# A latent RWKV kernel: its chains of two head pairs run half a chain apart, in double steps

## The chip, the cores and the metric

The kernel runs on one core of a Trainium2 chip. The metric is the device time of one launch in microseconds (us). The kernel before took 1387.38 us, the median of three runs (1385.10 to 1389.39). Its profile is of another execution, of 1384.0 us.

The engines are PE (matrix products), DVE (vector), ACT (scalar: functions and copies), POOL and SP (here mostly DMA queues). Each takes its instructions in the order in which they stand in its queue; semaphores tie the queues together.

## What is computed

Two layers of a diffusion backbone over 512 latent tokens of 1024 features, with 256 context tokens ahead. The part that matters is the first layer's time mixing, a recurrence over tokens run forwards and backwards, for 16 heads of 64:

```python
def wkv_scan(S0, r, decay, k, v, kk, a, reverse):
    def step(S, inp):
        r_t, w_t, k_t, v_t, kk_t, a_t = inp
        sa = jnp.einsum("bhvk,bhk->bhv", S, -kk_t)
        S = (S * w_t[:, :, None, :]
             + sa[..., None] * (kk_t * a_t)[:, :, None, :]
             + v_t[..., None] * k_t[:, :, None, :])
        return S, jnp.einsum("bhvk,bhk->bhv", S, r_t)
...
out_f, S_f = wkv_scan(S0_f, rt, tm(decay[0]), tm(kd[0]), vt, kkt, tm(a[0]), False)
out_b, S_b = wkv_scan(S0_b, rt, tm(decay[1]), tm(kd[1]), vt, kkt, tm(a[1]), True)
o = tm(out_f + out_b)
y = head_group_norm(o, lnx_w, lnx_b) + bonus
...
yb = bg * dwconv(cg * xb, sc_w, seg_len)
y = concat([ya * silu(za), yb * silu(zb)]) @ w_out
```

The starting states of the latent scan are the final ones of the same scan over the context. A gated short convolution (`yb`) runs beside it, and one output projection joins both.

## The kernel before

The recurrence is computed in chunks of 64 tokens, two heads (a pair) at a time, both directions z together. A pair goes through these parts, and the names are those of the code and of the profile's tiles:

- `light` (L506 on): per pair and direction, the decays and the scaled factors. Its tiles are sg, al, P and iP (running products of decays and their inverses), kd, bon, AR and BK, partly on ACT, partly on DVE. AR holds two kinds of chunk in turn, A (for the state's own correction) and R (for the output).
- `heavy` (L666 on): the products within chunks, pal, masked into E (DVE, L686); the transposes BKt (ACT, L699); Nt, copied out of E (ACT, L705); UV, into which v goes first.
- `solve` (L729 on): the inverse of a triangular 32 x 32 block, for all chunks at once: a transpose of Nt into Xl (L737), then 62 dependent DVE operations L743 and L745 on X and Y, in turn.
- `merge` (L748 on): two transposes of Y (kdm, am), copies into E, two bursts of 64 small matmuls (mg) with copies between. It makes the 64 x 64 inverses out of the halves.
- `chain_lat` (L836 on): the steps over the eight chunks, one chunk from the front (forwards) and one from the back (backwards) in each. A step takes the states H through six hops: matmuls zol (A H, with products of E and UV begun a step earlier) and onl (R H, the outputs), a copy of zol by ACT (L865), matmuls uh with E's inverses, a copy into UV by ACT (L872), matmuls uh with BKt, and the new H on DVE (L879) from them and HP, the scaled old state that ACT makes (L833). Then the outputs are finished and moved into the tile O, by a copy on ACT (L888) in the first four steps and an add on DVE (L891) in the last four.
- `finish` (L902 on): group norm of O, gate, and the projection's input.

The eight latent pairs are stages s = 4 to 11; a stage's parts are written by the letters in `STAGE[2]`, "OSPLMHFC", after the eight steps of pair s: po(s+1), solve(s+1), prep of s+2, light(s+2), merge(s+1), heavy(s+2), finish(s), and the convolution branch (four projections of 24 matmuls each: cg, xb, bg, zb). A list scheduler in the build orders each engine's instructions by what is ready and by their place in the program; `tc.issue_after` ties the parts of light, heavy and the convolution behind named steps of the running chain (`LIGHT_AFTER`, `HEAVY_AFTER`, `CONV_AFTER`, counted by `st["anchor"]`). `pinned()` (L641 on) keeps a run of matmuls in written order. So in the kernel before one pair's eight single steps and the next pair's solve are in the same stage.

After stage 11 comes the output projection (tiles wr, wh, wl, o) and the second layer, which the change does not touch.

PSUM has eight banks. The chain's use of them is `uh` (one bank, `uhs[0]`, for all pairs) and three rotating ones from `ps_zo` (two of tag zo, and uh1), which also serve merge and finish.

Of the kernel before, what the change touches and what calls it, by code (L numbers as in the profile page):

```python
# [51 lines left out]
def kernel(ctx: ExitStack, tc: tile.TileContext, I: dict, out: bass.AP):  # L52
# [176 lines left out]
    def start():  # L229
# [499 lines left out]
    def solve(st):  # L729
# [44 lines left out]
    def chain_ctx(st, i):  # L774
# [60 lines left out]

    def chain_lat(st, i):  # L836
        nm, p = st["nm"], st["p"]
        UV, E, BKt, AR, PC = st["UV"], st["E"], st["BKt"], st["AR"], st["PC"]
# [26 lines left out]
        S.copy(Zs, zo[:, 0:2, :])  # L865
        ahead = values(i + 1) if i < nch - 1 else []
        for h, z in hz:
            cmm(uh[ZR[1 - h], z, :], E[ZR[1 - h], h, z * nch + cs[z], 0:CH], Zs[ZR[1 - h], z, :])
            if ahead:
                ahead.pop(0)()  # L870
        for h in range(2):
            u_ = S.copy(UV[ZR[1 - h], i : 2 * nch - i : 2 * nch - 1 - 2 * i, ZR[h]], uh[ZR[1 - h], 0:2, :])  # L872
        h_ = None
        if i < nch - 1:
            for h, z in hz[::-1]:
                cmm(uh[ZR[h], 2 + z, :], BKt[z][:, cs[z], ZR[h]], UV[:, z * nch + cs[z], ZR[h]])
            Hn = w("H", f"H{nm}_{i}")[:, 0:P].rearrange("p (z x) -> p z x", z=2)
            for z in range(2):
                h_ = V.scalar_tensor_tensor(out=Hn[:, z, :], in0=uh[:, 2 + z, :],  # L879
                                            scalar=PC[z][:, i : i + 1], in1=HP[:, z, :], op0=ALU.mult, op1=ALU.add)  # L880
# [4 lines left out]
        for h, z in hz:
            cmm(on[ZR[h], oc[z], :], E[:, h, z * nch + cs[z], CH:], UV[:, z * nch + cs[z], ZR[h]], False, z == 1)
        if i < nch // 2:
            S.copy(O[:, i : nch - i : nch - 1 - 2 * i, :], on[:, 2:4, :])  # L888
        else:
            o = O[:, nch - 1 - i : i + 1 : 2 * i + 1 - nch, :]  # L890
            V.tensor_tensor(out=o, in0=on[:, 2:4, :], in1=o, op=ALU.add)  # L891
# [576 lines left out]
```

## Time and profile before

| what | value |
|---|---|
| median of three runs | 1387.38 us |
| profiled execution | 1384.0 us, span 1382.2 us |
| granted PE clock, mean | 0.992 |
| PE busy | 1319.8 us (95%) |
| DVE busy | 986.4 us (71%) |
| ACT busy | 744.4 us (54%) |
| the latent stages | about 484 to 872 us of the span |
| output projection and second layer | from about 872 us |

The span is what the trace covers; the execution's own time is 1.8 us longer. Times in rows of the timeline are us from the span's start; then the duration, the engine, the line, the operation, what it writes and reads, and its shape. In brackets stands the idle time of the engine ahead of it and what ended it. Matmuls are pipelined and their ends are modelled, so starts say more than ends. A window's row gives each engine's busy time, the number of its instructions in brackets, the granted clock, and the DMA engines' share.

### The profile page before, as it was taken

Reading aid. Unit: us, or ns where it says so; the run is one execution under the profiler, and the core shown is the slowest. Engines: PE = TensorE matmul, PEld = TensorE weight load, DVE = VectorE, ACT = ScalarE, POOL = GpSimd, SP = SyncE. Lnnn points to the kernel's source line nnn. Section 1 sums busy time; section 2 is a strip of 40 time slices with the busy share of each in tenths; the row PEclk is TensorE's granted clock in tenths of the full one; section 3 lists DMA queues with packets and bytes.
Section 4 is the critical chain, followed back from the end, with each engine's and each line's share of the span. In section 5 each row is a group of like instructions: output and inputs, shape, how many; then the busy total and the mean of one; then the engine's idle time right before and its main releaser. Section 6 shows DMA issues by size and latency. Waiting matters only on the chain.

```text
span 1382.2 us, 29703 instructions
## 1 busy us (share of the span) xinstructions
PE 1319.8 (95%) x11925; PEld 975.1 (71%) x11925; DVE 986.4 (71%) x2304; ACT 744.4 (54%) x1509; POOL 127.7 (9%) x263
## 2 busy tenths in 40 slices
PE   6999999999998999999999989999999999999998
PEld 2657777777666766666666666677777787788886
DVE  5857879867999499999999998458653653644323
ACT  6546476555765476675756755547742432554222
POOL 4142200001101010101101000010000000000000
PEclk9999999999999999999999999999999999999999
DMA  9865522222323322223222221578621321133232
GB/s 334 272 215 198 161 62 75 92 75 77 96 86 88 97 76 73 78 66 86 77 72 78 76 72 48 187 264 284 203 70 53 122 74 49 62 116 98 92 99 84
DMA packets 139754, 158.54 MB, mean 115 GB/s; under 512 B 15503, under 2 KB 104223, under 8 KB 139497
## 3 DMA queue, kind: packets, MB, share of 16 engines
q1 hardware_dynamic: 123152, 106.47, 24.9%
q0 software_dynamic: 15856, 49.12, 10.9%
q8 instruction: 93, 1.52, 0.5%
q10 hardware_dynamic: 608, 1.06, 0.2%
q14 instruction: 45, 0.37, 0.1%
HBM read 138.33 MB, written 18.28 MB: 113 GB/s over the span
## 4 chain that ended last, share of the span: by engine, by line
PE 46%; DVE 12%; ACT 7%; issue 4%; DMA 4%; POOL 0%; SPq 0%; DVEq 0%; ACTq 0%; POOLq 0%
PE pu L57 12%; PE pz L57 6%; PE f L57 6%; PE pxb L57 3%; PE pcg L57 3%; PE uh L57 3%; PE o L57 2%; DVE E L686 2%; DMA wr<-in_ev_w_out_dram 2%; PE pzb L57 1%; PE zol L57 1%; PE onl L57 1%; PE px L57 1%; PE pc L57 1%; DVE Yl L745 1%
## 5 line engine op out<-in xcount | busy, mean ns | idle before, releaser
L57 PE MATMUL o<-wh,y 128*128 128x512 f32 x248 | 79.8, 396 | 0.0
L743 DVE TENSOR_TENSOR xtmpl<-Xl,Yl 128x126 f32<-128x126 f32 (+22 forms) x248 | 62.3, 251 | 3.1
L745 DVE TENSOR_TENSOR Yl<-Yl,xtmpl 128x126 f32<-128x126 f32 (+22 forms) x248 | 62.2, 251 | 2.9
L1281 ACT CAST ah<-a 64x512 fp32r<-64x512 f32 x32 | 19.8, 618 | 74.8 <-DVE a L1276 74.4
L57 PEld LDWEIGHTS uh<-UV,BKt 128*64 128x64 f32 x704 | 26.4, 136 | 37.6 <-ACT UV L872 27.8
L57 PEld LDWEIGHTS o<-wh,y 128*128 128x128 f32 x248 | 46.2, 188 | 9.5
L57 PE MATMUL pal<-ARl,BKl 64*128 64x128 f32 x512 | 44.5, 295 | 8.7 <-DVE E L686 7.3
L57 PE MATMUL o<-wl,y 128*128 128x512 f32 x124 | 49.7, 401 | 2.3 <-DVE wl L130 2.3
L872 ACT COPY UV<-uh 64x128 f32<-64x128 f32 x128 | 33.3, 260 | 28.9 <-PE uh L57 26.6
L57 PEld LDWEIGHTS pal<-ARl,BKl 64*128 64x128 f32 x512 | 35.3, 191 | 18.8 <-issue 11.1
L130 DVE TENSOR_TENSOR wl<-wr,wh 128x1024 fp32r<-128x1024 f32 x28 | 34.2, 1223 | 19.1 <-ACT wh L129 19.0
L1276 DVE TENSOR_TENSOR a<-pu,a 128x512 f32<-128x512 f32 x16 | 11.0, 691 | 50.0 <-PE pu L57 47.7
L57 PE MATMUL uh<-UV,BKt 128*64 128x64 f32 x704 | 36.5, 232 | 8.7 <-ACT UV L872 4.5
L686 DVE TENSOR_TENSOR E<-pal,maskE 128x512 f32<-128x512 f32 x64 | 42.9, 684 | 0.3
L1233 DVE SCALAR_TENSOR_TENSOR pr<-px,dbe,What 119x512 f32<-119x512 f32 x32 | 22.6, 746 | 26.6 <-PE px L57 26.6
L129 ACT CAST wh<-wr 128x1024 fp32r<-128x1024 f32 x28 | 29.6, 1056 | 19.3 <-DMA wr<-in_ev_w_out_dram 10.1
L57 PEld LDWEIGHTS uh<-Ol,E 64*64 64x64 f32 x512 | 20.3, 133 | 25.8 <-ACT Ol L865 23.6
L879 DVE SCALAR_TENSOR_TENSOR Hl<-uh,PCl,HPl 128x64 f32<-128x64 f32 x112 | 26.2, 276 | 13.7 <-PE uh L57 5.2
L833 ACT ACTIVATE HPl<-Hl,PCl 128x64 f32<-128x64 f32 x96 | 28.1, 340 | 11.0 <-DVE Hl L879 9.8
L745 DVE TENSOR_TENSOR Yc<-Yc,xtmpc 128x126 f32<-128x126 f32 (+22 forms) x124 | 31.5, 254 | 3.1
L743 DVE TENSOR_TENSOR xtmpc<-Xc,Yc 128x126 f32<-128x126 f32 (+22 forms) x124 | 31.5, 254 | 3.0
L57 PEld LDWEIGHTS zol<-Hl,ARl 64*64 64x64 f32 x448 | 18.0, 134 | 21.0 <-DVE xtmpl L743 5.4
(1002 smaller groups left out, 4284.1 us busy)
## 6 DMA issues: line engine op xcount, KB each, us to landing
wr<-in_ev_w_out_dram SPq DMA_DIRECT2D x28, 512.0 KB, 5.2
mwr<-in_mod_w_dram POOLq DMA_DIRECT2D x28, 256.0 KB, 4.2
wrv<-in_ev_w_in_dram SPq DMA_DIRECT2D x16, 256.0 KB, 2.9
ectx<-in_mod_w_dram POOLq DMA_DIRECT2D x16, 256.0 KB, 4.4
wrr<-in_ev_w_in_dram SPq DMA_DIRECT2D x16, 256.0 KB, 2.9
wrza<-in_ev_w_in_dram SPq DMA_DIRECT2D x16, 256.0 KB, 2.8
wrcg<-in_ev_w_in_dram SPq DMA_DIRECT2D x16, 256.0 KB, 2.9
wrxb<-in_ev_w_in_dram SPq DMA_DIRECT2D x16, 256.0 KB, 2.9
```

The costliest lines, as they stand in the source:

```text
L57: env["pe"] = T.matmul(o, lhsT, rhs, start=start, stop=stop)
L129: S.copy(hi, raw)
L130: env["lo"].tensor_tensor(out=lo, in0=raw, in1=hi, op=ALU.subtract)
L686: st["ev"].append(V.tensor_tensor(out=E[:, h, z * NLAT + c0 : z * NLAT + c0 + m, :], in0=pas[h], in1=maskE[:, z * (1 + h) : z * (1 + h) + ...
L743: V.tensor_tensor(out=tv, in0=X[:, :i, i : i + 1].to_broadcast([P, i, m]), in1=Y[:, i : i + 1, c0:].to_broadcast([P, i, m]), op=ALU.mult)
L745: V.tensor_tensor(out=Y[:, :i, c0:], in0=Y[:, :i, c0:], in1=tv, op=ALU.add)
L833: S.activation(t[:, z, :], H[:, z, :], AF.Copy, scale=st["PC"][z][:, i : i + 1])
L872: u_ = S.copy(UV[ZR[1 - h], i : 2 * nch - i : 2 * nch - 1 - 2 * i, ZR[h]], uh[ZR[1 - h], 0:2, :])
L879: h_ = V.scalar_tensor_tensor(out=Hn[:, z, :], in0=uh[:, 2 + z, :], scalar=PC[z][:, i : i + 1], in1=HP[:, z, :], op0=ALU.mult, op1=ALU.add)
L1233: V.scalar_tensor_tensor(out=pr[s][:NPROD], in0=px[s][:NPROD], scalar=dbe[:, 0:1], in1=What[:, n * 512 : n * 512 + 512], op0=ALU.add, op1= ...
L1276: V.tensor_tensor(out=a, in0=pp[1], in1=a, op=ALU.mult)
L1281: S.copy(ahl[s][hr], a[hr])
```

## The change

The chains of two neighbouring pairs now run together, half a chain apart. Stage 4 first runs four single steps of pair 0 alone. Then each stage's letters are "OSMXPLHFC": solve(s+1) and merge(s+1) first, then X, which is four double steps: the steps 4 to 7 of pair s beside the steps 0 to 3 of pair s+1. Stage 11 ends with four single steps of the last pair.

`chain_lat` becomes a generator that yields between its hops, and `together` takes its two generators in turn, so the two pairs' instructions alternate in the program hop by hop. All its matmuls go through one `pinned()` list, `lat2["go"]`, which fixes their order on PE.

Each of the two pairs has, by its parity, two banks of its own: X (zol's sums, one of the `uhs`) and Y (one of the two zo banks, kept for the whole stretch; tiles zy). Y holds the second product uh in columns 0 and 1, the state product in 2 and 3, and the outputs in 4 and 5. H has two tiles and HP one, each split in halves by parity. The outputs of a step are computed and moved out in the next step (`closing`), ahead of that step's uh matmuls. The tile O is gone: AR becomes one tile for both directions (three buffers of twice the size in place of six), and the copies Zs and the outputs are written into the chunks of it that have been used. `merge` of a later pair works in the solve's X and Y tiles in place of kd, a and P, and in the bank that is the pair's X. Small tiles elsewhere that borrowed AR's buffers (tok, dh, wk1, we) are cut out of the wider tile.

```diff
-STAGE = ("KLSMVHvF", "OPLSMHF", "OSPLMHFC")
+STAGE = ("KLSMVHvF", "OPLSMHF", "OSMXPLHFC")
...
-    NBUF = {"tmp": 3, "bon": 3, "AR": 6, "BK": 2, "BKt": 4, "UV": 2, "E": 2, "PC0": 4, "PC1": 4, "rnq": 2,
+    NBUF = {"tmp": 3, "bon": 3, "AR": 3, "BK": 2, "BKt": 4, "UV": 2, "E": 2, "PC0": 4, "PC1": 4, "rnq": 2,
...
+        if st["lat"] and st["p"]:
+            Xt, Yt = st["XY"]
+            R1, R2, Gs = (t.rearrange("p (a b) -> p a b", b=32) for t in (Xt[:, 0:512], Xt[:, 512:], Yt))
...
-        pg = px = ps_zo("mg" + nm)
+        pg = px = uhs[1 - st["p"] % 2] if st["lat"] else uhs[1]
...
+    lat2 = {"go": pinned()}
...
+            st["py"] = lat2["y"][par]
+            st["xy"] = ch3(uhs[1 - par]), ch3(lat2["y"][par])
+            *st["hn"], st["hp"] = [t[:, par * P : par * P + P].rearrange("p (z x) -> p z x", z=2) for t in lat2["h"]]
...
+        def outs(i, H):
+            cs = (i, nch - 1 - i)
+            oc = (4, 5) if i < nch // 2 else (5, 4)
+            first = [(lambda h=h, z=z: go(Y[ZR[h], oc[z], :], AR[z][ZR[h], cs[z], CH:], H[ZR[h], z, :], z == 1, False))
+                     for z in (1, 0) for h in (1, 0)]
+            then = [(lambda h=h, z=z: go(Y[ZR[h], oc[z], :], E[:, h, z * nch + cs[z], CH:],
+                                         UV[:, z * nch + cs[z], ZR[h]], False, z == 1)) for h, z in hz]
+
+            def evict():
+                if i < nch // 2:
+                    S.copy(Q[:, 2 * i + 1 : 32 - 2 * i : 30 - 4 * i, :], Y[:, 4:6, :])
+                else:
+                    o = Q[:, 15 - 2 * i : 18 + 2 * i : 2 + 4 * i, :]
+                    V.tensor_tensor(out=o, in0=Y[:, 4:6, :], in1=o, op=ALU.add)
...
+        yield
+        Zs = Q[:, 2 * i : 31 - 2 * i : 30 - 4 * i, :]
+        S.copy(Zs, X[:, 0:2, :])
+        yield
+        closing([], then, evict)
+        yield
         ahead = values(i + 1) if i < nch - 1 else []
...
+    def together(*steps):
+        run = [chain_lat(st, i) for st, i in steps]
+        while run:
+            run = [g for g in run if next(g, run) is not run]
...
+        elif s == 4:
+            for i in range(NLAT // 2):
+                together((st, i))
         if s == 11:
+            for i in range(NLAT // 2, NLAT):
+                together((st, i))
             finish(st)
             break
...
+            elif x == "X":
+                for i in range(NLAT // 2):
+                    together((st, i + NLAT // 2), (sts[s + 1], i))
```

The order of DVE's queue before, inside the stage in which pair 3's chain runs. Hl is the new state; xtmpl, Xl and Yl belong to the solve of the next pair; rnql, rrl, kkl and Pl are light's.

```order
L745 TENSOR_TENSOR Yl_8155<-Yl_8155,xtmpl_8156 128x17x8
L502 TENSOR_TENSOR rnql_8244<-rnql_8244 128x16
L879 SCALAR_TENSOR_TENSOR Hl_1_7942<-uh_125,PCl_6600,HPl_1_7909 128x64
L879 SCALAR_TENSOR_TENSOR Hl_1_7942<-uh_125,PCl_6629,HPl_1_7909 128x64
L743 TENSOR_TENSOR xtmpl_8156<-Xl_8154,Yl_8155 128x128
L503 TENSOR_TENSOR rnql_8244<-rnql_8244 128x16
L745 TENSOR_TENSOR Yl_8155<-Yl_8155,xtmpl_8156 128x16x8
L504 SCALAR_TENSOR_TENSOR rnql_8244<-rnql_8244 128x16
L743 TENSOR_TENSOR xtmpl_8156<-Xl_8154,Yl_8155 128x135
L562 STREAM_TRANSPOSE rrl_8256<-rnql_8244 128x512
L745 TENSOR_TENSOR Yl_8155<-Yl_8155,xtmpl_8156 128x15x9
L565 SCALAR_TENSOR_TENSOR kkl_8258<-kl_8222,cols_68,rrl_8256 128x512
```

The same engine after, at the end of the solve of pair 3 (line numbers are those of the changed code: Hl is L920, the outputs' add L878, the merge L755 to L774, light's scan L599). zy_5339 is the bank Y of pair 2, in its second half, and zy_5340 that of pair 3.

```order
L745 TENSOR_TENSOR Yl_7075<-Yl_7075,xtmpl_7076 128x16
L755 STREAM_TRANSPOSE Xl_7074<-Yl_7075 128x32x16
L756 STREAM_TRANSPOSE Xl_7074<-Xl_7074 128x512
L760 COPY E_4885<-Xl_7074 32x16x32 x2
L769 COPY Yl_7075<-uh_125 32x512
L774 COPY E_4885<-uh_125 32x16x32
L920 SCALAR_TENSOR_TENSOR Hl_5341<-zy_5339,PCl_5916,HPl_5343 128x64
L920 SCALAR_TENSOR_TENSOR Hl_5341<-zy_5339,PCl_5945,HPl_5343 128x64
L920 SCALAR_TENSOR_TENSOR Hl_5341<-zy_5340,PCl_6717,HPl_5343 128x64
L920 SCALAR_TENSOR_TENSOR Hl_5341<-zy_5340,PCl_6746,HPl_5343 128x64
L599 SCALAR_TENSOR_TENSOR Pl_7542<-scm,sg 128x528
L878 TENSOR_TENSOR ARl_5923<-zy_5339,ARl_5923 128x2x64
```

The state rows have moved from between the solve's rows to behind the merge, in fours, and the rows beside them are light's wide ones.

ACT's queue before, around two steps of a chain (HPl, then the copy Ol of zol, then UV; al, kdl, iPl, Pl, PCl are light's):

```order
L833 ACTIVATE HPl_5_8891<-Hl_4_8888,PCl_7438 128x64
L833 ACTIVATE HPl_5_8891<-Hl_4_8888,PCl_7467 128x64
L865 COPY Ol_8713<-zol_5_8873 128x128
L610 ACTIVATE kdl_9145<-al_9136,oka,hka 128x512
L603 ACTIVATE iPl_9140<-Pl_9138 128x512
L872 COPY UV_4160<-uh_125 64x2x64 x2
L604 ACTIVATE Pl_9138<-Pl_9138 128x528
L606 COPY PCl_9143<-Pl_9138 128x8
L833 ACTIVATE HPl_6_8927<-Hl_5_8924,PCl_7438 128x64
L833 ACTIVATE HPl_6_8927<-Hl_5_8924,PCl_7467 128x64
```

ACT's queue after, the second double step of X with pairs 3 and 4 (L899 is the copy Zs, L875 the outputs' copy, L910 the copy into UV):

```order
L837 ACTIVATE HPl_5343<-Hl_5341,PCl_7518 128x64
L837 ACTIVATE HPl_5343<-Hl_5341,PCl_7547 128x64
L899 COPY ARl_6724<-uh_125 128x2x64
L899 COPY ARl_7525<-uh_126 128x2x64
L595 ACTIVATE al_8341<-lal_8338,hcol 128x512
L875 COPY ARl_7525<-zy_5339 128x2x64
L601 ACTIVATE iPl_8345<-Pl_8343 128x512
L910 COPY UV_4884<-zy_5340 64x2x64 x2
L602 ACTIVATE Pl_8343<-Pl_8343 128x528
L910 COPY UV_4143<-zy_5339 64x2x64 x2
L604 COPY PCl_8348<-Pl_8343 128x8
L608 ACTIVATE kdl_8350<-al_8341,oka,hka 128x512
```

Two pairs' copies now stand in one step, and light's four wide rows stand between them as they stood between one pair's.

More of the change, by code (lines that the diff above doesn't have):

```diff
@@ L249, in start @@
         dft = w("xtmp", "dft")[:31, :NPROD]
-        tokt = [w("AR", f"tok{j}") for j in range(6)]
+        tokt = [t[:, D * j : D * j + D] for t in [w("AR", f"tok{j}") for j in range(3)] for j in range(2)]
         for j in range(6):
@@ L786, in values @@
         def values(i):
-            st["zo"] = zo = ps_zo(f"zo{nm}_{i}")
+            st["zo"] = zo = ps.tile([P, 512], F32, tag="zo", name=f"zo{nm}_{i}", bufs=2)
             return [(lambda k=k, z=z, c=c, h=h: cmm(four(zo)[ZR[1 - h], k, :], E[ZR[h], h, z * NLAT + c, :],
@@ L834, in scale_H @@
         return t
+    lat2 = {"go": pinned()}
     def chain_lat(st, i):
-        nm, p = st["nm"], st["p"]
+        p, nch = st["p"], NLAT
         UV, E, BKt, AR, PC = st["UV"], st["E"], st["BKt"], st["AR"], st["PC"]
-        uh, nch = ch3(uhs[0]), NLAT
         if i == 0:
+            par = p % 2
+            if "y" not in lat2:
+                lat2["y"] = [ps.tile([P, 512], F32, tag="zo", name=f"zy{x}", bufs=2) for x in range(2)]
+                lat2["h"] = [w(t, f"{t}l{x}") for x, t in enumerate(("H", "H", "HP"))]
+            st["py"] = lat2["y"][par]
+            st["xy"] = ch3(uhs[1 - par]), ch3(lat2["y"][par])
+            *st["hn"], st["hp"] = [t[:, par * P : par * P + P].rearrange("p (z x) -> p z x", z=2) for t in lat2["h"]]
@@ L851, in values @@
             cs = (i, nch - 1 - i)
-            return [(lambda h=h, z=z: cmm(zo[ZR[1 - h], z, :], E[ZR[h], h, z * nch + cs[z], 0:CH],
-                                          UV[ZR[h], z * nch + cs[z], ZR[h]], z == 0, False)) for h, z in hz]
+            return [(lambda h=h, z=z: go(X[ZR[1 - h], z, :], E[ZR[h], h, z * nch + cs[z], 0:CH],
+                                         UV[ZR[h], z * nch + cs[z], ZR[h]], z == 0, False)) for h, z in hz]
+        def outs(i, H):
[8 more added lines that the diff above has]
+                    S.copy(Q[:, 2 * i + 1 : 32 - 2 * i : 30 - 4 * i, :], Y[:, 4:6, :])
+                else:
+                    o = Q[:, 15 - 2 * i : 18 + 2 * i : 2 + 4 * i, :]
+                    V.tensor_tensor(out=o, in0=Y[:, 4:6, :], in1=o, op=ALU.add)
+            return first, then, evict
@@ L855, in chain_lat, with closing @@
+        def closing(first, then, evict):
+            for f in first + then:
+                f()
+            evict()
         if i == 0:
-            for go in values(0):
-                go()
-        zo, on = st["zo"], ch3(ps_zo(f"on{nm}_{i}"))
+            for f in values(0):
+                f()
+        first, then, evict = st.get("outs") or ([], [], lambda: None)
         for z in (1, 0):
             for h in range(2):
-                m0_ = cmm(zo[ZR[1 - h], z, :], AR[z][ZR[h], cs[z], 0:CH], H[ZR[h], z, :], False, z == 0)
-                cmm(on[ZR[1 - h], oc[z], :], AR[z][ZR[1 - h], cs[z], CH:], H[ZR[1 - h], z, :], z == 1, False)
+                m0_ = go(X[ZR[1 - h], z, :], AR[z][ZR[h], cs[z], 0:CH], H[ZR[h], z, :], False, z == 0)
+                if first:
+                    first.pop(0)()
@@ L869, in chain_lat @@
             if ahead:
                 ahead.pop(0)()
+        yield
         for h in range(2):
-            u_ = S.copy(UV[ZR[1 - h], i : 2 * nch - i : 2 * nch - 1 - 2 * i, ZR[h]], uh[ZR[1 - h], 0:2, :])
+            u_ = S.copy(UV[ZR[1 - h], i : 2 * nch - i : 2 * nch - 1 - 2 * i, ZR[h]], Y[ZR[1 - h], 0:2, :])
         h_ = None
+        yield
+        st["outs"] = outs(i, H)
         if i < nch - 1:
             for h, z in hz[::-1]:
-                cmm(uh[ZR[h], 2 + z, :], BKt[z][:, cs[z], ZR[h]], UV[:, z * nch + cs[z], ZR[h]])
@@ L877, in chain_lat @@
-            Hn = w("H", f"H{nm}_{i}")[:, 0:P].rearrange("p (z x) -> p z x", z=2)
+                go(Y[ZR[h], 2 + z, :], BKt[z][:, cs[z], ZR[h]], UV[:, z * nch + cs[z], ZR[h]])
+            yield
+            Hn = st["hn"][i % 2]
             for z in range(2):
-                h_ = V.scalar_tensor_tensor(out=Hn[:, z, :], in0=uh[:, 2 + z, :],
+                h_ = V.scalar_tensor_tensor(out=Hn[:, z, :], in0=Y[:, 2 + z, :],
                                             scalar=PC[z][:, i : i + 1], in1=HP[:, z, :], op0=ALU.mult, op1=ALU.add)
@@ L883, in chain_lat @@
                 st["HP"] = scale_H(st, Hn, i + 1)
+        else:
+            closing(*st["outs"])
         st.setdefault("anc", []).append([x.ins for x in (m0_, u_, h_) if x is not None])
[L885 to L891, printed above, removed]
+    def together(*steps):
+        run = [chain_lat(st, i) for st, i in steps]
+        while run:
+            run = [g for g in run if next(g, run) is not run]
     def gate(p, cb, nm):
@@ L1123, in early @@
         else:
-            hl = [w(tag, f"we{k}{x}", F32R) for x in "hl"]
+            t = w(tag, f"we{k}", F32R)
+            hl = [t[:, x * D : x * D + D] for x in range(2)]
         return y, yr, [w("BK", f"wre{k}")[:, 0:D]] + hl
```

52 lines of the change are left out of this document (23 added, 29 removed).

## The prediction, before the result was known

> **What bounds the kernel now.** The page first, for the engines' totals and for what lies around the span.
>
> ```profile
> span 1382.2 us, 29703 instructions
> PE 1319.8 (95%) x11925; PEld 975.1 (71%) x11925; DVE 986.4 (71%) x2304; ACT 744.4 (54%) x1509; POOL 127.7 (9%) x263
> ```
>
> PE looks like the bound, but that is a mean over unlike stages. The change touches the eight latent head pairs, so next come the transposes of `solve` (one opens each pair's solve; tile Xl), which give the period of a stage, and then the busy time in windows cut at them.
>
> ```profile
> L737 DVE STREAM_TRANSPOSE Xl<-Nt x6: 1975/2025/2084, 528.4 to 820.2; 128x1024 f32<-128x1024 f32 x6
> core 0: us, PE busy (x) PEld busy (x) DVE busy (x) ACT busy (x) POOL busy (x), PEclk, DMA share, GB/s
> 484.50:528.40 43.90, 42.18 (x496) 28.76 (x496) 41.90 (x142) 29.25 (x74) 4.04 (x8) 1.00 0.23 68
> 528.40:820.20 291.80, 275.00 (x4019) 191.59 (x4020) 275.35 (x790) 188.42 (x447) 30.90 (x56) 1.00 0.26 75
> 820.20:872.00 51.80, 49.64 (x716) 33.81 (x716) 39.67 (x117) 25.82 (x67) 2.60 (x5) 0.97 0.20 61
> 872.00:911.00 39.00, 38.62 (x484) 25.97 (x480) 23.33 (x54) 23.10 (x61) 1.09 (x2) 1.00 0.63 204
> ```
>
> Six transposes make five periods of 291.80 / 5 = 58.4 us. DVE is busy for 275.35 / 5 = 55.1 of each and idle for 3.3. Its queue is what the stage costs: PE's 94% is mostly small matmuls whose modelled ends overlap. After 820 DVE falls to 77% and then 60%, and PE takes over (38.62 of 39.00).
>
> Third, what DVE is busy with: the solve's chain of dependent pairs, alone and with something between.
>
> ```profile
> 660.27 0.29 DVE L745 TENSOR_TENSOR Yl<-Yl,xtmpl 128x126 f32<-128x126 f32 x1
> 660.48 0.17 DVE L503 TENSOR_TENSOR rnql<-rnql 128x16 f32<-128x16 f32 x1
> 660.59 0.30 DVE L743 TENSOR_TENSOR xtmpl<-Xl,Yl 128x136 f32<-128x136 f32 x1
> 710.35 0.26 DVE L743 TENSOR_TENSOR xtmpl<-Xl,Yl 128x100 f32<-128x100 f32 x1
> 710.65 0.26 DVE L745 TENSOR_TENSOR Yl<-Yl,xtmpl 128x100 f32<-128x100 f32 x1
> ```
>
> An independent neighbour starts 0.08 before the end of the operation ahead of it (660.27 + 0.29 against 660.48); a dependent one 0.04 after it (710.61 against 710.65). Fourth, one step of a latent chain, which in the kernel before runs between such rows.
>
> ```profile
> 658.75 0.27 PE L57 MATMUL zol<-Hl,ARl 64*64 64x64 f32 x1
> 659.26 0.27 ACT L865 COPY Ol<-zol 128x128 f32<-128x128 f32 x1 [0.23 <-PE zol L57]
> 659.80 0.27 PE L57 MATMUL uh<-Ol,E 64*64 64x64 f32 x1
> 660.31 0.53 ACT L872 COPY UV<-uh 64x128 f32<-64x128 f32 x2 [0.78 <-PE uh L57]
> 660.89 0.45 PE L57 MATMUL uh<-UV,BKt 128*64 128x64 f32 x8
> 661.48 0.48 DVE L879 SCALAR_TENSOR_TENSOR Hl<-uh,PCl,HPl 128x64 f32<-128x64 f32 x2 [0.16 <-ACT sg L590]
> 662.04 0.59 ACT L833 ACTIVATE HPl<-Hl,PCl 128x64 f32<-128x64 f32 x2
> 662.17 0.27 PE L57 MATMUL zol<-Hl,ARl 64*64 64x64 f32 x1
> ```
>
> Six hops: 0.51 + 0.54 + 0.51 + 0.58 + 0.59 + 0.69 = 3.42 us, of which DVE works 0.48. Eight steps are far under 58.4, and the solve's rows stand in the gaps. So the chain's latency is hidden now; what a change must not do is leave DVE idle.
>
> **The change part by part.** *The count of DVE work* hardly moves: the order has 155 rows between two transposes before and after. So I take 55.1 us as a steady stage's work and ask where DVE idles. The rows shown with the change say it: before, the state rows (Hl) stand singly among solve rows; after, all solve rows come first, then the five merge rows with nothing between, then four double steps with only light's rows, then E rows and the transpose. The first half of the next pair's chain needs that merge, so X cannot start before it, and the next solve's rows stand behind X in DVE's queue. What the chain hid behind is gone.
>
> *A double step.* Two loops share ACT's queue and DVE's. The pair of H rows takes 0.48 and the next row starts 0.08 before its end; so with A's H at 0, B's is at 0.40, the four HP rows (0.59 a pair) run to 1.28 (as after 661.48), two Zs copies to 1.82, UV of A from 2.33 and of B to 3.39, B's BKt at 3.44 and its H at 4.03: 3.6 us bare, instead of 6.84 for two single steps. Light's rows stand in the same queues:
>
> ```profile
> 661.33 0.67 ACT L597 ACTIVATE al<-lal,hcol 128x512 f32<-128x512 f32 x1
> L610 ACT ACTIVATE kdl<-al,oka,hka 128x512 f32<-128x512 f32 x8 | 6.5, 813 | 0.0
> L604 ACT ACTIVATE Pl<-Pl 128x528 f32<-128x528 f32 x8 | 5.1, 644 | 0.1
> L637 ACT COPY BKl<-BKl 64x512 f32<-64x512 f32 x8 | 4.9, 617 | 0.1
> L601 DVE TENSOR_TENSOR_SCAN Pl<-scm,sg 128x528 f32<-128x528 f32 x8 | 10.0, 1254 | 0.3 <-ACT sg L593 0.2
> L891 DVE TENSOR_TENSOR Ol<-onl,Ol 128x128 f32<-128x128 f32 x16 | 4.5, 282 | 3.3 <-PE onl L57 3.3
> L686 DVE TENSOR_TENSOR E<-pal,maskE 128x512 f32<-128x512 f32 x32 | 21.2, 685 | 0.2
> ```
>
> First step: sg (as al, 0.67) between the two UV copies, less slack, 4.0. Second: al, the outs' copy (0.27) and iP (as P, 0.64) ahead of A's UV, P ahead of B's: +1.7, 5.3. Third: kd's 0.81 delays HP, and three wide DVE rows stand ahead of the out add, for which, as both use one bank, A's next uh matmul waits (it did not have to, with `on` in a bank of its own): +1.2, 4.8. Fourth: BK's 0.62 between the Zs copies, 4.3. X is 18.4. DVE's work in it: seven pairs of H at 0.40, 2.8; scan 1.2; four out adds 1.1; nine wide rows, as E 0.685 less the 0.08 that neighbours share, 5.4: together 10.5. **Idle in X: 7.9.**
>
> *The merge.* Its rows as they stand before, with others between:
>
> ```profile
> 687.36 1.11 DVE L751 STREAM_TRANSPOSE kdml<-Yl 128x512 f32<-128x512 f32 x1
> 688.98 0.71 DVE L752 STREAM_TRANSPOSE aml<-kdml 128x512 f32<-128x512 f32 x1
> 689.72 0.85 DVE L756 COPY E<-kdml 32x512 f32<-32x512 f32 x2
> 689.83 1.20 PE L57 MATMUL mgl<-aml,E 32*32 32x32 f32 x64 [0.30 <-DVE aml L752]
> 691.98 0.70 DVE L765 COPY Pml<-mgl 32x512 f32<-32x512 f32 x1
> ```
>
> With nothing between them, DVE waits for each of the two mgl bursts: 1.20 less the 0.85 of copies, and 1.20 again, with 0.1 at four hand-overs: **1.9 idle**.
>
> *The transpose's wait.* Nt is copied after the last E; on DVE, weights' and finish's rows stood between.
>
> ```profile
> 701.16 2.50 ACT L705 COPY Nt<-E 32x512 f32<-32x512 f32 x4 [1.55 <-DVE E L686]
> 703.69 1.98 DVE L737 STREAM_TRANSPOSE Xl<-Nt 128x1024 f32<-128x1024 f32 x1 [0.49 <-ACT Nt L705]
> ```
>
> The last two or three of the four copies follow the last E: some 2 us of the 2.50, in which one row of 0.6 stays as cover: **1.4 idle**. *Lost neighbours:* in the order of a stage a solve row follows the other directly 33 times, where it did 11 to 21 times, so some 17 lose the row between. With it the pair went at 0.32 (660.27 to 660.59); alone at 0.30, and the 0.17 row costs 0.17 less 0.08 elsewhere: 0.07 more, 0.09 for the larger tile: **1.5**. [...]
>
> Sum: 7.9 + 1.9 + 1.4 + 1.5 = 12.7 of idle where 3.3 was, a stage of 55.1 + 12.7 = 67.8, **+9.4, five times: +47**.
>
> *The first stage* (484.50 to 528.40): DVE's 41.90 gets what now comes ahead of the next transpose, eight H (1.7) and the merge (4.1 by the rows above, its last copy as Pml): 47.7 + 12.7 = 60.4, **+16.5**.
>
> *The tail* from 820.2: X runs there once without light, and four of the last pair's steps leave the output projection, where PE is full. About 1 us of PE a step (0.27 + 0.27 + 0.45 and overlaps) against X's waits of some 2 us: **-2**, bounds -6 and +4.
>
> Edits at nothing: one AR tile for both directions (same bytes), merge on Xt and Yt (dead after the solve), fixed order of the chain's matmuls (PE waits for ACT there anyway; if not, a matmul of 0.40 is late).
>
> Sum: 47 + 16.5 - 2 = +62 on the profiled execution's 1384.0 (1382.2 of span and 1.8 around it, taken as unchanged), that is 1446. It lies 3.4 under the median 1387.38, so **1449** as a median.
>
> **The rivals.** *Milder:* every double step bare (4 x 3.6, idle 3.9), the merge covered, no lost neighbours: 55.1 + 3.9 + 1.4 = 60.4, five times +2.0, the first stage 47.7 + 5.3 = 53, +9, tail -6: 1387.4 + 13 = 1400. It needs light's ACT rows to fall between the hops.
>
> *Faster:* the double step removes DVE's waits instead of adding some. If a double step is no longer than DVE's work in it (10.5 / 4 = 2.6 us), X idles nothing; with merge and transpose covered, a stage is 55.1 and gives -3.3 six times and -4 in the tail, 1387.4 - 24 = 1363; half of that is 1375. It decides at 2.6 us for two steps; one alone has 3.42 of hops. For it speaks that ACT, whose rows lengthen three of the four steps, is free for a third of the stage (188.42 of 291.80 busy).
>
> *The clock.* This chain-only stretch of before has one, with the H rows on either side:
>
> ```profile
> 827.00:830.40 3.40, 2.09 (x36) 1.49 (x36) 3.13 (x10) 2.53 (x7) 0.08 (x1) 0.98 0.07 22
> 830.40:833.90 3.50, 3.50 (x38) 1.93 (x36) 2.74 (x10) 0.87 (x4) 1.00 (x2) 0.53 0.51 152
> 828.32 0.27 PE L57 MATMUL uh<-Ol,E 64*64 64x64 f32 x1 [1.31 <-ACT Ol L865]
> 829.99 0.48 DVE L879 SCALAR_TENSOR_TENSOR Hl<-uh,PCl,HPl 128x64 f32<-128x64 f32 x2
> 835.31 0.47 DVE L879 SCALAR_TENSOR_TENSOR Hl<-uh,PCl,HPl 128x64 f32<-128x64 f32 x2 [1.97 <-PE uh L57]
> ```
>
> After 3.4 us at 61% PE the granted clock was 0.53, and the step took 5.3 us, 1.9 over the 3.42 of the step above. X has PE about half busy for 18 us. Halved throughout it would cost 1.9 x 4 steps x 6 stages = 46; as the low stretch here ends after 3.5 us, I price three steps in four: +34, 1483. For it, that row; against it, double steps bring twice the matmuls. The Trainium skill (TensorE: Matmul & The Clock Gate, "Why this matters for your kernels") asks only for no idle gap over some 3 us; by that the clock stays whole, yet here it halved with 1.31 us as the idle time before that matmul.
>
> *Not half a chain apart:* A's wait for the out add, or ACT's order, makes the pairs run one after the other: 6.84 a step, X 27.4, idle 16.9 + 4.8, a stage 76.8: five times +18.4, the first +25.5, tail -2, 1503.
>
> **How the numbers follow.** Forecast 0.65, milder 0.11, clock 0.10, one after the other 0.03, faster 0.07, no change by offsets I don't see 0.04. The range runs from the milder case, 1400, to the clock's, 1483; the rest outside is 0.14 and some of each edge. A measurement of this kernel tells 0.3% (4 us) from no change. Faster 0.07, within 0.04, slower 0.89.
>
> **What would show it.** Transposes 67.8 us apart (64 to 71); DVE idle in X near 8 us, released by PE's zy matmuls and ACT's UV; a double step of 4 to 5.3, H to H; the first transpose after the first chain near 545; clock whole in X. A period under 60 makes the prediction wrong: then rows from beside X fill it, or double steps are under 3 us.

## The result, and the profile after

The changed kernel takes 1541.25 us, the median of four runs (1531.00 to 1545.66), against 1387.68 for the kernel before (four runs). The ratio is 1.1108, with a 95% interval of 1.1051 to 1.1165: 154 us slower, where +62 was forecast and 1483 was the upper end. The profiled execution took 1531.0 us. Its page, in the first lines and the row of the granted clock in 40 slices:

```profile
span 1529.2 us, 29756 instructions
PE 1368.5 (89%) x11925; PEld 1039.4 (68%) x11925; DVE 1004.6 (66%) x2304; ACT 749.2 (49%) x1509; POOL 128.0 (8%) x263
PEclk9999999989999787776868795969999999999999
```

The clock row is the news. Before, it was 9 throughout; now it falls to between 5 and 8 in most slices of the latent stages (from the 14th to the 27th). The transposes that open the solves, and the window between the first and the last of them:

```profile
L737 DVE STREAM_TRANSPOSE Xl<-Nt x6: 2046/2056/2059, 566.1 to 964.0; 128x1024 f32<-128x1024 f32 x6
566.10:964.00 397.90, 305.62 (x3860) 230.95 (x3859) 283.83 (x780) 190.63 (x444) 30.21 (x54) 0.77 0.18 53
```

Five periods are 397.9 us, 79.6 each, in place of 58.4. Five times 21.2 is 106 of the 147 us by which the span grew. The stage ahead of them (from the first H at 491.45 to 566.1) grew from 43.9 to 74.7, +31; what lies before the first H, which the change hardly touches, +7 in this execution (e3 below, with the same program up to there, has its first H at 483.8, where it was before); the tail +3.

DVE's work in a period is 283.83 / 5 = 56.8 (55.1 before); its idle time is 22.8 where 12.7 was forecast. One stage, cut at its phases: the solve's last part (657 to 679), the merge, the wait for the first H, the double steps, and the rest:

```profile
657.00:667.00 10.00, 10.00 (x45) 7.87 (x44) 10.00 (x35) 6.83 (x12) 0.49 (x1) 1.00 0.37 108
667.00:674.00 7.00, 2.38 (x11) 1.65 (x9) 6.82 (x19) 2.05 (x4) 0.00 (x0) 0.86 0.24 68
674.00:679.30 5.30, 0.00 (x0) 0.00 (x0) 4.68 (x20) 0.00 (x0) 0.00 (x0) 0.50 0.20 58
679.30:687.70 8.40, 3.84 (x128) 3.57 (x128) 3.95 (x6) 2.38 (x4) 0.54 (x1) 0.50 0.01 2
687.70:692.00 4.30, 3.56 (x64) 2.89 (x64) 0.01 (x1) 1.84 (x6) 0.00 (x0) 0.50 0.22 61
692.00:698.20 6.20, 5.65 (x100) 4.61 (x100) 3.05 (x8) 5.61 (x19) 0.54 (x1) 0.50 0.04 13
698.20:706.70 8.50, 8.29 (x113) 6.31 (x113) 4.88 (x13) 3.60 (x12) 1.60 (x3) 0.50 0.26 73
706.70:714.70 8.00, 7.80 (x110) 5.55 (x111) 2.61 (x8) 3.65 (x12) 2.38 (x4) 0.60 0.18 57
714.70:727.00 12.30, 11.82 (x122) 8.77 (x121) 11.07 (x28) 4.99 (x10) 0.57 (x1) 1.00 0.14 44
```

Read the columns of PE and the clock together. From 669.4 to 681.1 PE has nothing to do, and the clock goes to half at 672 (read in windows of 1 us). It stays there through the merge and X until 713, although PE is 91 to 98% busy in the last 20 us of that. X (687.7 to 714.7) takes 27.0 us, DVE works 10.55 of them. In PE's timeline, the two bursts of the merge with PE's last row ahead of them:

```profile
669.00 0.39 PE L57 MATMUL pxb<-hlh,wlxb 128*128 128x512 f32 x1
681.12 1.92 PE L57 MATMUL uh<-Xl,E 32*32 32x32 f32 x64 [11.74 <-DVE Xl L756]
684.45 1.92 PE L57 MATMUL uh<-Xl,Yl 32*32 32x32 f32 x64 [1.41 <-DVE Yl L769]
```

The convolution's projection xb has ended 12 us before the merge's first burst. A burst that took 1.20 takes 1.92. The merge and the double steps on DVE:

```profile
679.26 1.06 DVE L755 STREAM_TRANSPOSE Xl<-Yl 128x512 f32<-128x512 f32 x1
687.02 0.69 DVE L774 COPY E<-uh 32x512 f32<-32x512 f32 x1 [2.63 <-ACT E L774]
692.02 0.48 DVE L920 SCALAR_TENSOR_TENSOR Hl<-zy,PCl,HPl 128x64 f32<-128x64 f32 x2 [4.31 <-PE zy L57]
698.17 0.47 DVE L920 SCALAR_TENSOR_TENSOR Hl<-zy,PCl,HPl 128x64 f32<-128x64 f32 x2
706.69 0.48 DVE L920 SCALAR_TENSOR_TENSOR Hl<-zy,PCl,HPl 128x64 f32<-128x64 f32 x2 [2.25 <-PE zy L57]
708.04 0.48 DVE L920 SCALAR_TENSOR_TENSOR Hl<-zy,PCl,HPl 128x64 f32<-128x64 f32 x2 [0.88 <-PE zy L57]
714.72 0.47 DVE L920 SCALAR_TENSOR_TENSOR Hl<-zy,PCl,HPl 128x64 f32<-128x64 f32 x2
```

The merge takes 8.45 us (forecast 6.0 by its terms). The steps of the older pair, from H to H, take 6.2 and 8.5, those of the newer one (693.3, 699.6, 708.04, 714.72) 6.3, 8.5 and 6.7, and DVE waits for PE.

### The profile page after: what moved, and what is told of

Its sections match the earlier page's. It is cut to its first block, busy times and chain, and to the rows that moved or that the text cites. A ratio compares the mean times of both kernels' runs of the same rounds, so it can differ in the third digit from the quotient of the medians.

```text
span 1529.2 us, 29756 instructions
## 1 busy us (share of the span) xinstructions
PE 1368.5 (89%) x11925; PEld 1039.4 (68%) x11925; DVE 1004.6 (66%) x2304; ACT 749.2 (49%) x1509; POOL 128.0 (8%) x263
## 4 chain that ended last, share of the span: by engine, by line
PE 49%; DVE 14%; ACT 6%; issue 4%; DMA 4%; POOL 0%; SPq 0%; DVEq 0%; ACTq 0%; POOLq 0%
PE pu L57 12%; PE zy L57 6%; PE pz L57 6%; PE f L57 6%; PE uh L57 4%; PE pcg L57 3%; DVE xtmpl L743 2%; PE pxb L57 2%; DVE Yl L745 2%; PE o L57 2%; PE pzb L57 2%; PE pal L57 2%; DMA wr<-in_ev_w_out_dram 1%; DVE E L686 1%; ACT UV L910 1%
## 5 line engine op out<-in xcount | busy, mean ns | idle before, releaser
L57 PE MATMUL uh<-Xl,E 32*32 32x32 f32 x448 | 13.4, 237 | 72.9 <-DVE Xl L756 72.9
L920 DVE SCALAR_TENSOR_TENSOR Hl<-zy,PCl,HPl 128x64 f32<-128x64 f32 x112 | 26.5, 278 | 63.7 <-PE zy L57 55.5
L57 PEld LDWEIGHTS uh<-Xl,E 32*32 32x32 f32 x448 | 12.5, 151 | 75.8 <-DVE Xl L756 75.8
L57 PE MATMUL pal<-ARl,BKl 64*128 64x128 f32 x512 | 53.2, 328 | 5.3 <-DVE E L686 5.0
L910 ACT COPY UV<-zy 64x128 f32<-64x128 f32 x128 | 33.3, 260 | 27.4 <-PE zy L57 25.7
L57 PE MATMUL uh<-UV,E 64*64 64x64 f32 x512 | 34.7, 294 | 9.8 <-DVE E L774 9.8
L57 PE MATMUL zy<-UV,BKt 128*64 128x64 f32 x448 | 33.9, 296 | 7.4 <-ACT UV L910 7.3
L705 ACT COPY Nt<-E 32x512 f32<-32x512 f32 x32 | 19.8, 617 | 40.8 <-DVE E L686 40.5
L57 PEld LDWEIGHTS zy<-UV,BKt 128*64 128x64 f32 x448 | 25.0, 190 | 19.9 <-ACT UV L910 14.9
L57 PEld LDWEIGHTS zy<-ARl,E 64*64 64x64 f32 x512 | 26.0, 186 | 15.7 <-ACT ARl L875 7.1
```

The lines of the kernel that those rows point to most:

```text
L57: env["pe"] = T.matmul(o, lhsT, rhs, start=start, stop=stop)
L705: S.copy(Nt[rs], E[rs, h, :, 32 * b : 32 * b + 32])
L920: h_ = V.scalar_tensor_tensor(out=Hn[:, z, :], in0=Y[:, 2 + z, :], scalar=PC[z][:, i : i + 1], in1=HP[:, z, :], op0=ALU.mult, op1=ALU.add)
```

## The experiments

Two theories stood at the start. *Clock:* the halved clock makes X PE-bound; whole, the stage would be near the forecast 67.8. *Order:* X and the merge stand bare in the queues, and the clock is a side effect.

**The clock, with work that isn't needed.** e3 adds 39 matmuls of 128x512 per stage, three behind each of the last 13 adds of the solve, into a bank that nobody reads; nothing is left out.

```diff
+    def warm(st):
+        t = ps_mm(f"dum{st['nm']}")
+        for x in st["sv"][FROM:]:
+            with tc.issue_after(x.ins):
+                for k in range(PER):
+                    e = mm(t, hlat[0][:, 0, 0:P], hlat[0][:, 1, :], True, True)
+                    if k == 0:
+                        tc.add_manual_dep(e.ins, x.ins.name, ...)
```

> The changed kernel with 39 further matmuls of 128x512 per stage (into a bank nobody reads), three behind each of the last 13 of the solve's 31 adds, so that PE has work until the merge. Clock theory: the 11.7 us in which PE had nothing halve the clock, and X at half clock is bound by PE; kept whole, the merge takes 6 to 7 us in place of 8.4 and X 18 to 21 in place of 27.2, the period falls from 79.6 to 69 to 73 and the time to 1470 to 1495. Rival, order alone: clock or not, the hops and ACT's queue set X; the time stays within 1% of 1541. Third: X's small matmuls can't hold the clock by themselves; then it falls within X again and the period is 74 to 78.

Measured: 1479.55, ratio 1.0676 (1.0637 to 1.0714), clock 0.984. Its transposes, the windows of the filling, the merge and X, and a stretch within X:

```profile
L738 DVE STREAM_TRANSPOSE Xl<-Nt x6: 2041/2050/2055, 552.9 to 914.6; 128x1024 f32<-128x1024 f32 x6
650.00:657.00 7.00, 7.00 (x23) 5.15 (x22) 6.28 (x23) 0.41 (x1) 0.00 (x0) 0.70 0.14 40
657.00:666.00 9.00, 9.00 (x158) 6.95 (x157) 3.22 (x6) 3.01 (x5) 0.54 (x1) 1.00 0.06 10
666.00:677.00 11.00, 10.28 (x237) 7.67 (x236) 6.37 (x16) 9.07 (x30) 0.53 (x1) 1.00 0.15 49
677.00:686.00 9.00, 7.71 (x159) 5.66 (x156) 7.45 (x17) 5.86 (x20) 3.98 (x7) 1.00 0.51 149
671.30:677.40 6.10, 5.78 (x144) 4.55 (x144) 4.85 (x11) 5.67 (x20) 0.66 (x2) 1.00 0.04 13
```

The period is 361.7 / 5 = 72.3, within the expectation, and the clock is whole from the merge to X's end. With it the loss falls from 154 to 94 us: some 60 hang on the clock. But xb's matmuls had moved too, from the solve into the merge and the first part of X, so this run alone can't say which of the large matmuls held the clock. In the last row none of 128x512 starts, and the clock stays whole: there X's small matmuls hold it by themselves.

**The filling alone.** e5 puts 24 such matmuls into the bank of the next merge, so that xb stays ahead.

> As e3, but 24 filling matmuls, two behind each of the last 12 adds of the solve, into the bank that the next merge will use, so that xb stays where it was (in e3 its matmuls had moved into the merge and X). With a whole clock the prediction's sum has a period of 67.8 and 1449; e3's 72.3 would then come from xb standing in the merge. If its 72.3 is what X costs at a whole clock, this stays at 71 to 73 and 1475 to 1485. If 24 are too few to hold the clock, 75 or more.

Measured: 1515.39, ratio 1.0951 (1.0923 to 1.0979), period 77.6, the last of its three cases. The merge and X's beginning, the middle of X, two windows of a later stage, and PE around the clock's fall:

```profile
674.00:678.00 4.00, 2.87 (x72) 2.12 (x70) 2.90 (x5) 1.81 (x3) 0.00 (x0) 1.00 0.02 4
678.00:682.00 4.00, 2.25 (x81) 2.02 (x81) 0.99 (x2) 0.57 (x1) 0.54 (x1) 0.74 0.22 48
686.50:692.80 6.30, 6.23 (x104) 4.96 (x102) 3.02 (x8) 5.47 (x17) 0.53 (x1) 0.50 0.04 13
836.90:847.20 10.30, 7.78 (x153) 6.40 (x153) 3.09 (x7) 6.58 (x20) 1.07 (x2) 0.50 0.11 34
847.20:851.00 3.80, 3.66 (x80) 2.96 (x80) 2.94 (x8) 3.42 (x13) 0.49 (x1) 1.00 0.01 4
675.75 1.20 PE L58 MATMUL uh<-Xl,E 32*32 32x32 f32 x64
678.36 1.20 PE L58 MATMUL uh<-Xl,Yl 32*32 32x32 f32 x64 [1.41 <-DVE Yl L771]
680.95 0.69 PE L58 MATMUL uh<-UV,E 64*64 64x64 f32 x8 [1.40 <-DVE E L776]
```

The clock was whole when the merge's first burst began and was lost within 6 us of small matmuls, with no gap above 1.41; PE is busy for 72% and then 56% of the first two windows. So a busy solve's end is not enough. Whether the small matmuls or the many short gaps lose the clock is not told apart here.

The fourth of e5's five stages goes another way. It too loses the clock in the merge, but at 847.2, in the second double step, the clock is whole again, though no matmul of 128x512 has run since 833 and none does until 851. This stage takes 73.5 us (798.5 to 871.9, from transpose to transpose), the other four 78.5 to 78.9. So X at a mostly whole clock gives a stage near e3's 72.3 also where xb has not moved.

**The kernel's own large matmuls.** e4 ties the projections cg and xb to later adds of the solve; e12 ties cg to one of them, and xb to the older pair's step 4. Nothing is added. Both edits change one line, shortened here, with the anchors of the convolution's cg, xb, zb and bg (sv: the adds of the next solve, from 0; an: the steps of the chain; e4 first, e12 second):

```diff
-                conv_branch(s - 3, st["anchor"])
+                conv_branch(s - 3, [sv[14].ins, 0, sv[22].ins, 0, 0, 0, an[6], an[7]])
...
+                conv_branch(s - 3, [sv[18].ins, 0, an[4], 0, 0, 0, an[6], an[7]])
```

> The changed kernel with the convolution's cg and xb projections tied behind the 15th and the 23rd of the solve's 31 adds, so that PE's own work reaches the solve's end; nothing is added. Clock theory: as with the filling matmuls, period 69 to 73, time 1470 to 1495. Order alone: within 1% of 1541.

> The changed kernel, double steps and common order kept, with cg tied behind the 19th of the solve's adds and xb behind the first double step: 128x512 matmuls of the kernel's own at the solve's end, in the merge and spread over X, and nothing added. e3 held a whole clock with xb there and 39 filling matmuls ahead; e4, with both projections ended before the merge, did not. If large matmuls within X are what holds the clock, it is whole or nearly so here, the period 71 to 74 and the time 1465 to 1490. If the filling matmuls at the solve's end held it, the clock halves here too and the time is 1500 or more.

Measured: e4 1514.49, ratio 1.0938 (1.0853 to 1.1023), clock 0.925, half in X; its expectation by the clock theory was missed. It filled the solve's end, with two last matmuls of xb in the merge (674.4), and lost the clock behind them, as e5 did. e12 1481.05, ratio 1.0684 (1.0644 to 1.0724), clock 0.951. Its transposes, its windows in X, and H:

```profile
L737 DVE STREAM_TRANSPOSE Xl<-Nt x6: 2039/2052/2061, 558.5 to 917.7; 128x1024 f32<-128x1024 f32 x6
679.00:684.00 5.00, 4.68 (x113) 3.43 (x109) 3.43 (x8) 4.93 (x17) 0.53 (x1) 1.00 0.05 16
684.00:689.00 5.00, 4.49 (x109) 3.44 (x109) 4.66 (x12) 3.76 (x14) 1.60 (x4) 1.00 0.24 66
689.00:694.00 5.00, 4.42 (x108) 3.32 (x104) 4.27 (x11) 3.57 (x13) 2.37 (x4) 1.00 0.66 199
678.07 0.48 DVE L921 SCALAR_TENSOR_TENSOR Hl<-zy,PCl,HPl 128x64 f32<-128x64 f32 x2 [3.73 <-ACT sg L588]
679.34 0.47 DVE L921 SCALAR_TENSOR_TENSOR Hl<-zy,PCl,HPl 128x64 f32<-128x64 f32 x2 [0.79 <-PE zy L57]
683.60 0.96 DVE L921 SCALAR_TENSOR_TENSOR Hl<-zy,PCl,HPl 128x64 f32<-128x64 f32 x4
688.76 1.03 DVE L921 SCALAR_TENSOR_TENSOR Hl<-zy,PCl,HPl 128x64 f32<-128x64 f32 x4 [0.33 <-ACT UV L911]
694.15 0.47 DVE L921 SCALAR_TENSOR_TENSOR Hl<-zy,PCl,HPl 128x64 f32<-128x64 f32 x2
```

Period 359.2 / 5 = 71.8. The clock dips in e12's merge (0.59 and 0.50) but is whole in X, and it is X that matters. At a whole clock the older pair's H rows are 5.5 and 5.2 us apart, the newer pair's (679.34, the second halves of the two joined rows, 694.15) 4.8, 5.2 and 4.8. e3 and e12 agree on what the order alone costs: a stage of 72, 1480 us.

The expectation was that large matmuls spread over X hold the clock there. The number came, but not that way. The matmuls of step 4 that xb is tied to, its first hop, run at 638.9, long before the merge; so xb comes right behind cg, and 14 of its 24 matmuls run in and just behind the merge (666.1 to 674.0). At 675 the clock is whole again, and only four of them start after 679. With e3's and e5's rows the reading is: what matters is that the clock is whole early in X. At a whole clock X's small matmuls hold it (144 of them in e3's 6.1 us). At half clock they run slower, PE looks as busy or busier (104 in 6.3 us, 99%), and in most stages they do not bring it back. That the half clock keeps itself up by the smaller number of matmuls is argued from these counts, not tested.

**Light ahead of X.** e6 is e5 with light's part written ahead of the merge (`"OSPLMXHFC"`, and light's own ties moved to fit), so that X holds only the chains.

> As e5, and the next pair's light is written ahead of the merge and X, so that X holds nothing but the two chains. The prediction's terms for light's rows in X (+0.4, +1.7, +1.2, +0.7) say that bare double steps take 3.6 each, X about 4 us less than in e5, and that DVE idles more there: a period near 70. If the double step is bound by its own hops and by ACT's and PE's queues, not by light, its steps stay at 4.5 or more and the period is 73 or more.

Measured: 1556.48, ratio 1.1257 (1.1224 to 1.1289), clock 0.919, period 85.2; X stood at a clock of 0.50. Neither theory of light's rows is tested at a whole clock, so that stays open. At the same half clock X, from the merge's last copy to the last H, takes 24.8 us here and 26.3 in e5, but the stage as a whole is longer, not shorter.

**What ties the order.** e2 runs X as four single steps of the older pair and then four of the newer. e8 keeps the double steps and changes one line: each pair has a fixed matmul order of its own.

```diff
-        go, H, HP = lat2["go"], st["H"], st["HP"]
+        go, H, HP = st.setdefault("go", pinned()), st["H"], st["HP"]
```

> The changed kernel, but X runs four single steps of the older pair and then four of the newer one, in place of four double steps. If a double step saves nothing over two single ones (PE-bound at half clock), the time stays within 2% of 1541. If pairing hides latency as meant, eight steps of about 5.3 us at half clock stand against 27 us now: some 42, a period near 95 us, 1620 or more.

> The changed kernel with one edit: the fixed matmul order is kept for each pair by itself, not for both together. The build then puts the older pair's last four steps beside the solve, as in e2, and only the newer pair's first four behind the merge. If the common order is what ties the older pair behind the merge, this falls from 1541 to about e2's 1412 (1400 to 1425). If the order of the program's parts ties it, it stays near 1541.

Measured: e2 1411.69, ratio 1.0171 (1.0126 to 1.0217); e8 1411.77, ratio 1.0202 (1.0156 to 1.0247). e2's expectation was wrong on both sides, as both took the place of the steps for given. e8's says why: without a common order the build moves the older pair's four steps into the solve. e2 keeps the one shared list, but in it the older pair's matmuls all stand ahead of the newer pair's, and the same thing happens. So what ties is not the list, but that the two pairs alternate in it. e8's transposes, and H around a merge:

```profile
L737 DVE STREAM_TRANSPOSE Xl<-Nt x6: 1970/2018/2083, 538.2 to 861.2; 128x1024 f32<-128x1024 f32 x6
735.14 0.47 DVE L920 SCALAR_TENSOR_TENSOR Hl<-zy,PCl,HPl 128x64 f32<-128x64 f32 x2
748.38 0.28 DVE L920 SCALAR_TENSOR_TENSOR Hl<-zy,PCl,HPl 128x64 f32<-128x64 f32 x1
766.22 1.17 DVE L755 STREAM_TRANSPOSE Xl<-Yl 128x512 f32<-128x512 f32 x1
779.30 0.47 DVE L920 SCALAR_TENSOR_TENSOR Hl<-zy,PCl,HPl 128x64 f32<-128x64 f32 x2 [1.18 <-PE zy L57]
```

H rows stand ahead of the merge again (735, 748); in the changed kernel there are none from the transpose to the merge. With the alternating order gone the loss is 27 us in place of 154: it is worth some 127 us, clock included. Only the newer pair's four steps stay bare, and the period is 64.6.

**The step code by itself.** e1 has the new step with the old order of a stage, eight single steps beside the solve. e7 adds to it a bank for the outputs that is not the one of uh and the state product (the other pair's Y, free in this order).

```diff
-            first = [(lambda h=h, z=z: go(Y[ZR[h], oc[z], :], ...
+            YO = ch3(lat2["y"][1 - p % 2])
+            first = [(lambda h=h, z=z: go(YO[ZR[h], oc[z], :], ...
...
-                    V.tensor_tensor(out=o, in0=Y[:, 4:6, :], in1=o, op=ALU.add)
+                    V.tensor_tensor(out=o, in0=YO[:, 4:6, :], in1=o, op=ALU.add)
```

> The new step code (own banks, outputs finished one step later, one AR tile, merge on the solve's tiles, one fixed matmul order) with the old order of a stage: eight single steps of one pair beside the next pair's solve, no X. If the order (X behind solve and merge) is what costs, this stands within 10 us of the kernel before, 1378 to 1398, with transposes 57 to 60 us apart and a whole clock in the stages. If the step code costs by itself (one bank for the states and the outputs, so a wait for the out add), it is 1400 or more.

> As e1 (old order, eight single steps), but the outputs' products go to the other pair's bank Y, so that the next uh matmul doesn't wait for the add or copy that empties them. If that wait is what e1 lost (13 us over the kernel before, steps of 4.2 to 5.1), it comes back to 1383 to 1391 and steps near 4.0. If not, it stays at 1395 to 1402.

Measured: e1 1398.92, ratio 1.0095 (1.0065 to 1.0124), between its two cases; e7 1382.81, ratio 0.9984 (0.9960 to 1.0009). e1's first and last H of a stage with an add of the outputs and the H rows on either side of it, then e7's first and last H:

```profile
668.59 0.48 DVE L920 SCALAR_TENSOR_TENSOR Hl<-zy,PCl,HPl 128x64 f32<-128x64 f32 x2
686.95 0.47 DVE L920 SCALAR_TENSOR_TENSOR Hl<-zy,PCl,HPl 128x64 f32<-128x64 f32 x2 [0.28 <-PE zy L57]
688.78 0.29 DVE L878 TENSOR_TENSOR ARl<-zy,ARl 128x128 f32<-128x128 f32 x1
691.20 0.47 DVE L920 SCALAR_TENSOR_TENSOR Hl<-zy,PCl,HPl 128x64 f32<-128x64 f32 x2
695.22 0.48 DVE L920 SCALAR_TENSOR_TENSOR Hl<-zy,PCl,HPl 128x64 f32<-128x64 f32 x2 [0.24 <-PE zy L57]
```

```profile
659.45 0.43 DVE L921 SCALAR_TENSOR_TENSOR Hl<-zy,PCl,HPl 128x64 f32<-128x64 f32 x2
682.50 0.48 DVE L921 SCALAR_TENSOR_TENSOR Hl<-zy,PCl,HPl 128x64 f32<-128x64 f32 x2 [0.15 <-PE zy L57]
```

In e7 six steps take 23.05 us, 3.84 each; in e1 the same six (668.59 to 695.22) take 4.44. The wait for the shared bank was the whole of e1's loss.

**A version that beats both?** e9 is e7 with the merge in its former tiles, e10 is e7 without the fixed order, e11 has both edits.

> As e7, and the merge works in the tiles kd, a and P again, so that the next solve's transpose needn't wait for the merge to leave Xl and Yl. If that wait (0.35 us and the merge's rows ahead of the first transpose in e7) is exposed, the time falls below e7's 1383 to 1374 to 1380; if the merge is only at another place of the same queue, it stays within 0.3%.

> As e7, without the fixed order of the chain's matmuls. If the fixed order costs (a matmul that is ready waits behind one that isn't), the time falls by 3 to 8 us; if the single steps are bound by their hops, it stays within 0.3% of e7; if the build then puts outputs ahead of state products, it gets slower by some us.

> Both edits of e9 and e10. The changes of e9 and e10 add up if they are in different places: 1370 to 1383. What then stays of the change is that outputs are finished one step later, AR in one tile and O gone; if that is worth anything, it shows here against the kernel before (1385), by more than 0.3%.

Measured: ratios 0.9983 (0.9965 to 1.0002), 0.9989 (0.9968 to 1.0010), 0.9982 (0.9965 to 0.9999), medians 1385.39, 1384.27 and 1385.38 against 1387.59. None is clear of the 0.3% below which a difference isn't told here, and e11's 1370 to 1383 was missed. The merge's tiles and the fixed order are at no cost where the steps stand beside the solve.

## Why the prediction was wrong, point by point

- **DVE's queue sets a stage; the solve stands alone, then merge, then X.** Right. DVE's work went from 55.1 to 56.8 a stage, and the 1.7 more is about the size of the term for lost neighbours (1.5). It shows as work and not as idle time: the solve's rows are as long as before (0.25 us on average), but a stage's rows, added up, overlap by some 8 us where they overlapped by 10.
- **X.** DVE's work in it was 10.5 by the sum and is 10.55. The length was the error: 18.4 forecast, 27.0 measured. At a whole clock it is 20.3 in e3 (from 665.6, where the merge's last copy ends, to the last H at 685.9), and its steps in e12 are 5.5 and 5.2 for the older pair and 4.8, 5.2 and 4.8 for the newer, where 5.3, 4.8 and 4.3 stood. So the walk through ACT's queue was short by some 2 us, and the other 6.7 are the clock, as far as xb's new place in e3 does not count.
- **The merge.** 1.9 of idle forecast, 8.4 - 3.95 = 4.45 measured: its bursts at half clock, 1.92 in place of 1.20 twice, and ACT's copy behind each burst, some 0.6, which DVE's own copy waits for and which the term left out. In e5, where the clock is whole until the merge's last copies, the merge takes 7.1.
- **The transpose's wait.** 1.4 forecast; 1.2 a stage in the changed kernel, 1.4 in e3 and e12.
- **The clock: the step that failed.** It stood as a rival with a chance of 0.10 and a price of 34 us, and "double steps bring twice the matmuls" was held against it. It is worth some 60 (a loss of 154 us against 94 in e3 and 96 in e12). Two things were wrong in it. The order is shown for DVE and ACT, the engines that wait, and not for PE, where cg and xb now end 12 us ahead of the merge's first burst. They are tied behind the older pair's steps 0 and 2, and these steps now lie in the stage before, so that this tie no longer holds the two back; in the kernel before, xb's matmuls ran from 670.1 to 686.0, up to the merge at 687.4. And the low stretch was priced by its length before, 3.5 us; between the first and the last transpose it now lasts 31 to 41 us a stage, since X's matmuls at half clock rarely bring the clock back, and PE becomes the bound in it. The price of a low X was near: 1.9 x 4 = 7.6 a stage, three quarters of it taken, which is 5.7, against 6.7 by e3. But the clock was kept out of the forecast, and its 1483 left out the low merge, and what the order cost beyond +62. The forecast's 1449, the 32 that the order was short and the 60 of the clock make 1541.
- **"X cannot start before the merge."** Half right. It holds for the newer pair's steps. The older pair's are tied only by the fixed matmul order in which the two pairs alternate, which the text had put among the edits at nothing. e8 prices it at some 127 us, the larger part of the loss. The +62 was thus worked out for the right place of the steps, but from a wrong reason for half of them.
- **The out add in the bank of uh.** Named, and real: some 15 us in single steps (e1 against e7, each against the kernel before).
- **The first stage.** +16.5 forecast, to 60.4; +31 measured, to 74.7. In e3, where the clock is low for 3.4 us of it, it takes 69.1 (483.8 to 552.9). So about 5.5 of the 14 us are the clock, and 8.7 the order.

The order alone, +94 by e3 and e12, is over the forecast's +62 by the walk through X, by a merge that waits longer, and by a first stage that no term took for long enough. By e3 the five stages have 5 x 4.5 (72.3 against 67.8) and the first stage 8.7 of the 32 us between. How the 4.5 of a stage divide stays open: in e3 X is 1.9 over its term and the merge, with xb's matmuls in it, 3.4.

## What to carry to other kernels

Before steps are taken out of a queue's gaps, ask what fills the gaps now: a chain that is hidden costs nothing, and pairing it saves nothing. A fixed order in which two streams alternate ties the one to whatever the other waits for; fix it for each stream. And read the changed order on the engine with the throttled clock too: see where its large matmuls end, and place some so that the clock is whole when a long run of small ones begins.

## What the runs showed of the hardware

In the changed kernel's stage shown, the granted clock stood at 0.50 for 41 us (672 to 713). In the last 20 of them PE was 91 to 98% busy, nearly all of it with matmuls of 64x64, 128x64 and 64x128; six of 128x512 from 703 on did not bring it back before 713. In e5 it went from 1.00 to 0.50 within 6 us, with no idle gap above 1.41 us. The Trainium skill (TensorE: Matmul & The Clock Gate, "Why this matters for your kernels") asks for no idle gap above some 3 us; by that the clock would have been kept in e5's merge, and it wasn't. Matmuls of 128x512 are not needed to hold it: in e3 it stayed at 1.00 for 6.1 us without one (671.3 to 677.4), and in e5's fourth stage it came back without one (847.2). What counts may be how much of the array the matmuls use in a given time, but that was not measured by itself. At half clock a burst of 64 matmuls of 32x32 takes 1.92 us in place of 1.20.
